# Smaller weight loads and separate tiles for the modulation sums in a hybrid encoder block

## The chip, the cores and the metric

The kernel runs on one core of a Trainium2 chip. The metric is the device time of one execution in microseconds; before the change it is the median of three runs.

## The reference

One encoder layer on 256 tokens of width 2048, in float32:

```python
mod = silu(c) @ ada_w + ada_b                 # c: (1, 2048), ada_w: (2048, 6*2048)
shift_m, scale_m, gate_m, shift_f, scale_f, gate_f = split(mod, 6)
h = rms_norm(x, norm_mix_w) * (1 + scale_m) + shift_m
proj = h @ w_in                               # 18512 columns
# branch A: bidirectional chunkwise mLSTM, 4 heads      -> y_a = (...) @ w_branch_a
# branch B: bidirectional gated delta rule, 16 heads    -> y_b = (...) @ w_branch_b
x = x + gate_m * ((g_a * y_a + g_b * y_b) @ w_out)
hf = rms_norm(x, norm_ffn_w) * (1 + scale_f) + shift_f
gt, up = split(hf @ w_gate_up, 2)             # 2 x 5632 columns
x = x + gate_f * ((silu(gt) * up) @ w_down)
return rms_norm(x, norm_final_w)
```

All weights together are some 450 MB, each read once. `mod` needs the whole of `ada_w`, six parts of 2048 x 2048, which are called here parts 0 to 5.

## The kernel before

**Products.** A float32 product is made of three passes: a weight tile `raw` is split into a rounded high part `wh` (on ScalarE) and the rest `wl` (on VectorE, `wl = raw - wh`), the activations likewise, and TensorE multiplies high with high, high with low and low with high. Two helpers do this. `fjob` takes 16 blocks of 128 x 128 weights as the stationary side and leaves the result with features on partitions (tiles `acc_b` and `acc_a`). `tjob` moves weights of 512 columns past stationary activations; it walks over chunks `u` of 4 x 128 rows in two halves `k0` (0 and 2), each of 12 matmuls. Both read their weights by loads of 1 MB on the SP queue into tiles with the tag `raw`, of which there are three; each such tile gives two halves. `wh` and `wl` have three tiles each, of half the size.

**Modulation sums.** Parts 0 and 1 of `mod` are made in the opening, by two loads `ra` of 1 MB for each of 16 blocks of rows, beside a weight load of 1 MB, `raw0`, which feeds the first 16 products (`first`, line 507). Parts 2 to 5 are made in the background by `ada_part`: a block of 128 x 2048 of the transposed `ada_w` is loaded and VectorE multiplies it with `silu(c)`, broadcast to all partitions (`row_c`), and sums over the row in the same instruction (line 124). Its tile also has the tag `raw`, so these loads and the weight loads share three tiles:

```python
for b in range(KB):
    raw = st.tile([P, D], F32, tag="raw", bufs=3, name=f"ada{part}_{b}")
    nc.sync.dma_start(raw, ada4[part - 2, b])
    V.scalar_tensor_tensor(raw, raw, 1.0, row_c[:, :D], ALU.mult, ALU.mult,
                           accum_out=mod[:, c0 + b : c0 + b + 1])
    yield True
```

**Order.** The Python program lays out the work as generators. `sums(n)` takes n steps of the background list; `pump()` is called by the jobs and calls `sums` every second or fourth time (`every[0]`), or not at all. `fills` holds projection jobs that are put between the short steps of the recurrent branches. The instructions then go through a planner, which may change their order on an engine except where `order(...)` keeps it; on the chip each engine, and the SP queue, runs its own list in order. A tile is given to its next user when the last reader of the user before has ended, so a load waits in the SP queue for the instruction that frees its tile. The stages in order of time (us from the start of the span): opening to about 130; gates; the delta rule's heads with the `b`, `a`, `z`, `v`, `o`, `m` projections as filling, to about 976; the mLSTM heads with the branch projections `yb` and `ya`, to about 1229; the output projection `o` (four groups `g` of 512 columns, with `residual`), to about 1328; the second normalisation, then the FFN: `gt` and `up` to about 1815, `d` to about 2040; the last normalisation.

In the output projection the steps of the background are written out by hand: at half `i` of group `g`, `sums()` is called if `i` is in a given list, and at `g == 3, i == 4` the rest is drained, since the second normalisation needs parts 3 and 4.

Of the kernel before, what the change touches and what calls it, by code (L numbers as in the profile page):

```python
# [15 lines left out]
P = 128  # L16
# [8 lines left out]
KD = 11  # L25
GRP = 4
N0 = 4 + 3 * GRP


PK_ADAB = 0  # L30
# [22 lines left out]
def hybrid_block(ctx: ExitStack, tc: tile.TileContext, xr, nfr, crow, pk_d, cst_d, ada2, ada4, win0, winb, wint, wba, wbb, wo, wgu, wd, out, dbg=None):  # L53
# [31 lines left out]
    def order(ins, yes=True):  # L85

        return tc.keep_in_program_order(ins) if yes else ins
# [6 lines left out]
    pk = cp.tile([P, PK_N], F32, name="pk")  # L94
    cst = cp.tile([P, CS_N], F32, name="cst")
    cp.tile([P, 20], F32, name="edge")
    c1 = st.tile([1, D], F32, tag="raw", bufs=3, name="c1")
    S.dma_start(c1, crow.unsqueeze(0))
    S.dma_start(cst, cst_d)
    S.dma_start(pk, pk_d)  # L100
    ident = cst[:, CS_ID : CS_ID + P]
# [9 lines left out]
    V.memset(row_c[:, D:], 1.0)  # L111
    def c_row(g):
        pc_ = acc_ps.tile([P, 512], F32, tag="acc", name=f"crow{g}")
        order(PE.matmul(pc_, ones[0:1], c1[:, g * 512 : (g + 1) * 512], start=True, stop=True))
        order(S.activation(row_c[:, g * 512 : (g + 1) * 512], pc_, AF.Silu))


    def ada_part(part, row_c):

        c0 = part * KB  # L120
        for b in range(KB):
            raw = st.tile([P, D], F32, tag="raw", bufs=3, name=f"ada{part}_{b}")
            nc.sync.dma_start(raw, ada4[part - 2, b])
            V.scalar_tensor_tensor(raw, raw, 1.0, row_c[:, :D], ALU.mult, ALU.mult, accum_out=mod[:, c0 + b : c0 + b + 1])  # L124
            yield True
        V.tensor_tensor(mod[:, c0 : c0 + KB], mod[:, c0 : c0 + KB], pk[:, PK_ADAB + c0 : PK_ADAB + c0 + KB], ALU.add)
        yield True


# [16 lines left out]
    def fjob(name, src, done):  # L146

        ps = acc_ps.tile([P, 512], F32, tag="acc", name=f"acc_{name}")
        o = ps[:, :T]
        raw = st.tile([P, KB, P], F32, tag="raw", bufs=3, name=f"raw_{name}")  # L150
        nc.sync.dma_start(raw, src)
        for k0 in range(0, KB, 8):
            wh = st.tile([P, 8, P], F32R, tag="wh", bufs=3, name=f"wh_{name}_{k0}")
            wl = st.tile([P, 8, P], F32R, tag="wl", bufs=3, name=f"wl_{name}_{k0}")
            S.activation(wh, raw[:, k0 : k0 + 8], AF.Copy)  # L155
            V.tensor_tensor(wl, raw[:, k0 : k0 + 8], wh.bitcast(F32), ALU.subtract)  # L156
            for k in range(8):
                kk = k0 + k
                PE.matmul(o, wh[:, k], both(hh, kk).rearrange("p a b -> p b a"), start=kk == 0, stop=False)  # L159
                PE.matmul(o, wh[:, k], both(hl, kk).rearrange("p a b -> p b a"), start=False, stop=False)  # L160
                PE.matmul(o, wl[:, k], both(hh, kk).rearrange("p a b -> p b a"), start=False, stop=kk == KB - 1)  # L161
            if k0:
                pump()
                done(o.rearrange("p (b a) -> p a b", a=2))
            yield True

    def tjob(name, chunks, xh, xl, done, early=0, by_token=None, steps=1):
# [1 line left out]

        raws = {}

        def halves(u, k0):
            if u not in raws:
                raws[u] = st.tile([P, 4, 512], F32, tag="raw", bufs=3, name=f"raw_{name}_{u}")
                nc.sync.dma_start(raws[u], chunks[u])
            wh = st.tile([P, 2, 512], F32R, tag="wh", bufs=3, name=f"wh_{name}_{u}_{k0}")
            wl = st.tile([P, 2, 512], F32R, tag="wl", bufs=3, name=f"wl_{name}_{u}_{k0}")
            order(S.activation(wh, raws[u][:, k0 : k0 + 2], AF.Copy), early)  # L180
            order(V.tensor_tensor(wl, raws[u][:, k0 : k0 + 2], wh.bitcast(F32), ALU.subtract), early)  # L181
            return wh, wl

        todo = [(u, k0) for u in range(len(chunks)) for k0 in (0, 2)]
# [9 lines left out]
        for n, (u, k0) in enumerate(todo):  # L194
            wh, wl = made.pop(0) if made else halves(u, k0)
            for k in range(2):
                kk = 4 * u + k0 + k
                for t in range(2):
                    order(PE.matmul(ps[t], tok(xh, kk, t), turns(wh[:, k]), start=kk == 0, stop=False), early and steps > 1)  # L199
                    PE.matmul(ps[t], tok(xl, kk, t), turns(wh[:, k]), start=False, stop=False)  # L200
                    PE.matmul(ps[t], tok(xh, kk, t), turns(wl[:, k]), start=False, stop=kk == last)  # L201
# [236 lines left out]
    with ExitStack() as s0:  # L438
# [54 lines left out]
        for b in range(KB):  # L493
            if b:
                ra, raw = loads(b)
                m2 = scale(b, ra)
            order(V.scalar_tensor_tensor(x[:, b], x[:, b], m2[:, 0:1], rows, ALU.mult, ALU.mult))
            if b:
                shift(ra, m2)
            order(S.activation(x[:, b], x[:, b], AF.Identity, bias=m2[:, 1:2]))  # L500
            two = lambda a: a.rearrange("p (a b) -> p a b", a=2)
            order(S.activation(both(hh, b), two(x[:, b]), AF.Copy))
            for bb in ((b - 1,) if b < KB - 1 else (b - 1, b)):
                if bb >= 0:
                    order(V.tensor_tensor(both(hl, bb), two(x[:, bb]), both(hh, bb).bitcast(F32), ALU.subtract))
            for o in range(N0):
                PE.matmul(  # L507
                    first[o], raw[:, o], x[:, b], start=b == 0 and o % 2 == 0, stop=b == KB - 1 and o % 2 == 1
                )


# [608 lines left out]
    for g in range(4):  # L1120
# [239 lines left out]
```

## Time and profile before

| | us |
|---|---|
| median of 3 runs (2050.05 to 2060.24) | 2050.77 |
| the profiled execution | 2056.24 |
| its span, first to last instruction | 2054.3 |
| mean granted TensorE clock | 0.986 |
| DMA moved, mean over the span | 236 GB/s |

The page gives for each engine the busy time and its share of the span, for stretches the clock that was granted to TensorE, for groups of instructions the mean duration and what ended the idle time before them, and for DMA issues the time from issue to landing. PE is TensorE, PEld its weight loads, DVE VectorE, ACT ScalarE, POOL GpSimd; SPq is the queue from which SP issues loads. "DVE x <- ACT y" means that VectorE's instruction on x waited for ScalarE's on y. L124 is line 124 of the kernel before.

### The profile page before, as it was taken

Reading aid. Unit: us, or ns where it says so; the run is one execution under the profiler, and the core shown is the slowest. Engines: PE = TensorE matmul, PEld = TensorE weight load, DVE = VectorE, ACT = ScalarE, POOL = GpSimd, SP = SyncE. Lnnn points to the kernel's source line nnn. Section 1 sums busy time; section 2 is a strip of 40 time slices with the busy share of each in tenths; the row PEclk is TensorE's granted clock in tenths of the full one; section 3 lists DMA queues with packets and bytes.
Section 4 is the critical chain, followed back from the end, with each engine's and each line's share of the span. In section 5 each row is a group of like instructions: output and inputs, shape, how many; then the busy total and the mean of one; then the engine's idle time right before and its main releaser. Section 6 shows DMA issues by size and latency. Waiting matters only on the chain.

```text
span 2054.3 us, 27035 instructions
## 1 busy us (share of the span) xinstructions
PE 1968.2 (96%) x10374; PEld 1707.0 (83%) x10374; DVE 1394.8 (68%) x2059; ACT 1054.0 (51%) x1584; POOL 106.1 (5%) x205
## 2 busy tenths in 40 slices
PE   8999989999998899999999999889999999999998
PEld 6777779988987898899878787678888888888886
DVE  5787777786888588765667778766656665555554
ACT  3147547856774677466443443364444444444443
POOL 0002210010101010100200000000000000000000
PEclk9999999999999999999999999999999999999999
DMA  9986664566765565666987578756766766555654
GB/s 400 420 321 211 173 216 146 173 190 221 240 224 178 194 207 211 232 247 241 361 295 263 211 264 315 271 184 240 255 243 245 254 238 221 192 204 204 205 203 143
DMA packets 78962, 485.64 MB, mean 236 GB/s; under 512 B 10585, under 2 KB 15969, under 8 KB 24433
## 3 DMA queue, kind: packets, MB, share of 16 engines
q1 hardware_dynamic: 63360, 450.95, 60.9%
q0 software_dynamic: 8160, 17.88, 4.0%
q10 hardware_dynamic: 7314, 15.10, 1.9%
q8 instruction: 81, 1.33, 0.3%
q14 instruction: 47, 0.39, 0.0%
HBM read 467.07 MB, written 16.82 MB: 236 GB/s over the span
## 4 chain that ended last, share of the span: by engine, by line
PE 67%; DVE 13%; DMA 11%; ACT 5%; issue 3%; POOL 1%; ACTq 0%; SPq 0%; DVEq 0%; POOLq 0%
PE acc_up L201 4%; PE acc_up L199 4%; PE acc_up L200 4%; PE acc_d L200 4%; PE acc_d L201 4%; PE acc_d L199 4%; PE acc_gt L200 3%; PE acc_gt L201 3%; PE acc_gt L199 3%; DMA ra<-ada 3%; PE acc_b L161 2%; PE acc_b L159 2%; PE acc_b L160 2%; DMA ada<-ada 2%; PE acc_yb L201 1%
## 5 line engine op out<-in xcount | busy, mean ns | idle before, releaser
L181 DVE TENSOR_TENSOR wl_d<-raw_d,wh_d 128x1024 fp32r<-128x1024 f32 x88 | 107.8, 1225 | 109.1 <-ACT wh_d L180 109.1
L181 DVE TENSOR_TENSOR wl_up<-raw_up,wh_up 128x1024 fp32r<-128x1024 f32 x88 | 107.7, 1225 | 100.4 <-ACT wh_up L180 100.4
L159 PE MATMUL acc_b<-hh,wh_b 128*128 128x256 f32 x576 | 164.1, 285 | 5.8 <-ACT wh_b L155 5.8
L181 DVE TENSOR_TENSOR wl_gt<-raw_gt,wh_gt 128x1024 fp32r<-128x1024 f32 x88 | 107.8, 1225 | 83.2 <-ACT wh_gt L180 83.2
L161 PE MATMUL acc_b<-hh,wl_b 128*128 128x256 f32 x576 | 161.7, 281 | 2.0 <-DVE wl_b L156 2.0
L124 DVE SCALAR_TENSOR_TENSOR ada<-ada,crow 128x2048 f32<-128x2048 f32 x64 | 146.4, 2287 | 25.0 <-DMA ada<-ada 24.8
L160 PE MATMUL acc_b<-hl,wh_b 128*128 128x256 f32 x576 | 160.4, 279 | 0.0
L180 ACT ACTIVATE wh_d<-raw_d 128x1024 fp32r<-128x1024 f32 x88 | 92.9, 1056 | 127.9 <-PE acc_d L200 119.2
L180 ACT ACTIVATE wh_gt<-raw_gt 128x1024 fp32r<-128x1024 f32 x88 | 92.9, 1056 | 118.6 <-PE acc_gt L200 71.0
L180 ACT ACTIVATE wh_up<-raw_up 128x1024 fp32r<-128x1024 f32 x88 | 92.9, 1055 | 108.9 <-PE acc_up L200 78.2
L199 PE MATMUL acc_gt<-wh_gt,hfh 128*128 128x512 f32 x352 | 135.4, 385 | 0.0
L200 PE MATMUL acc_gt<-wh_gt,hfl 128*128 128x512 f32 x352 | 134.7, 383 | 0.1
L201 PE MATMUL acc_gt<-wl_gt,hfh 128*128 128x512 f32 x352 | 133.7, 380 | 0.0
L199 PE MATMUL acc_up<-wh_up,hfh 128*128 128x512 f32 x352 | 133.5, 379 | 0.0
L201 PE MATMUL acc_up<-wl_up,hfh 128*128 128x512 f32 x352 | 133.5, 379 | 0.0
L200 PE MATMUL acc_up<-wh_up,hfl 128*128 128x512 f32 x352 | 133.5, 379 | 0.0
L200 PE MATMUL acc_d<-wh_d,ffl 128*128 128x512 f32 x344 | 131.0, 381 | 0.0
L199 PE MATMUL acc_d<-wh_d,ffh 128*128 128x512 f32 x344 | 131.0, 381 | 0.0
L201 PE MATMUL acc_d<-wl_d,ffh 128*128 128x512 f32 x344 | 130.5, 379 | 0.0
L507 PE MATMUL first<-x,raw 128*128 128x256 f32 x512 | 114.5, 382 | 7.4 <-ACT x L500 6.8
L159 PEld LDWEIGHTS acc_b<-hh,wh_b 128*128 128x128 f32 x576 | 112.5, 195 | 6.4 <-ACT wh_b L155 6.3
L507 PEld LDWEIGHTS first<-x,raw 128*128 128x128 f32 x512 | 96.1, 190 | 25.8 <-ACT x L500 12.4
(369 smaller groups left out, 5275.9 us busy)
## 6 DMA issues: line engine op xcount, KB each, us to landing
ada<-ada SPq DMA_DIRECT2D x64, 1024.0 KB, 5.0
raw_gt<-wgu SPq DMA_DIRECT2D x44, 1024.0 KB, 5.0
raw_up<-wgu SPq DMA_DIRECT2D x44, 1024.0 KB, 4.9
raw_d<-wd SPq DMA_DIRECT2D x44, 1024.0 KB, 4.9
raw_b<-winb SPq DMA_DIRECT2D x36, 1024.0 KB, 5.4
ra<-ada SPq DMA_DIRECT2D x32, 1025.0 KB, 15.7
raw<-win SPq DMA_DIRECT2D x16, 1024.0 KB, 14.5
raw_z<-wint SPq DMA_DIRECT2D x16, 1024.0 KB, 5.8
```

The lines of the kernel that those rows point to most:

```text
L124: V.scalar_tensor_tensor(raw, raw, 1.0, row_c[:, :D], ALU.mult, ALU.mult, accum_out=mod[:, c0 + b : c0 + b + 1])
L159: PE.matmul(o, wh[:, k], both(hh, kk).rearrange("p a b -> p b a"), start=kk == 0, stop=False)
L160: PE.matmul(o, wh[:, k], both(hl, kk).rearrange("p a b -> p b a"), start=False, stop=False)
L161: PE.matmul(o, wl[:, k], both(hh, kk).rearrange("p a b -> p b a"), start=False, stop=kk == KB - 1)
L180: order(S.activation(wh, raws[u][:, k0 : k0 + 2], AF.Copy), early)
L181: order(V.tensor_tensor(wl, raws[u][:, k0 : k0 + 2], wh.bitcast(F32), ALU.subtract), early)
L199: order(PE.matmul(ps[t], tok(xh, kk, t), turns(wh[:, k]), start=kk == 0, stop=False), early and steps > 1)
L200: PE.matmul(ps[t], tok(xl, kk, t), turns(wh[:, k]), start=False, stop=False)
L201: PE.matmul(ps[t], tok(xh, kk, t), turns(wl[:, k]), start=False, stop=kk == last)
L507: PE.matmul(first[o], raw[:, o], x[:, b], start=b == 0 and o % 2 == 0, stop=b == KB - 1 and o % 2 == 1)
```

## The change

Weights come in loads of 512 KB, one for each half, into four tiles `raw` of 512 KB (before, three of 1 MB). The modulation sums are made in halves of 1024 columns into `mh`, whose two columns are added at the end of a part together with the bias. Their tiles have the tag `ada`: two of 512 KB, and six in the pool of the output projection while that runs; the load of step n + 1 stands in the program ahead of the sum of step n. `pump()` is called after each half, so a step is half a sum at twice as many calls. The lists in the output projection go from 3 + 4 + 4 + 3 whole steps to 6 + 8 + 8 + 5 half steps. In the opening, `raw0` comes as two loads, the first into a `raw` tile, the second into a `wl` tile, and the row `c` as two loads. The tiles of these tags take 48 KB per partition before and after, outside the output projection's pool, which grows by 24 KB.

```diff
+NR = 4
+NW = 3
...
-    c1 = st.tile([1, D], F32, tag="raw", bufs=3, name="c1")
-    S.dma_start(c1, crow.unsqueeze(0))
+    c1 = [st.tile([1, D // 2], F32, tag="raw", bufs=NR, name=f"c1_{i}") for i in range(2)]
+    for i in range(2):
+        S.dma_start(c1[i], crow.unsqueeze(0)[:, i * D // 2 : (i + 1) * D // 2])
...
+    ada_in = [st, 2]
     def ada_part(part, row_c):
         c0 = part * KB
-        for b in range(KB):
-            raw = st.tile([P, D], F32, tag="raw", bufs=3, name=f"ada{part}_{b}")
-            nc.sync.dma_start(raw, ada4[part - 2, b])
-            V.scalar_tensor_tensor(raw, raw, 1.0, row_c[:, :D], ALU.mult, ALU.mult, accum_out=mod[:, c0 + b : c0 + b + 1])
+        mh = cp.tile([P, 2, KB], F32, tag="mh", bufs=1, name=f"mh{part}")
+        cols = [slice(i * D // 2, (i + 1) * D // 2) for i in range(2)]
+        def load(b, i):
+            raw = ada_in[0].tile([P, D // 2], F32, tag="ada", bufs=ada_in[1], name=f"ada{part}_{b}_{i}")
+            nc.sync.dma_start(raw, ada4[part - 2, b][:, cols[i]])
+            return raw
+        todo = [(b, i) for b in range(KB) for i in range(2)]
+        raw = load(*todo[0])
+        for n, (b, i) in enumerate(todo):
+            if n + 1 < len(todo):
+                ahead = load(*todo[n + 1])
+            V.scalar_tensor_tensor(raw, raw, 1.0, row_c[:, cols[i]], ALU.mult, ALU.mult, accum_out=mh[:, i, b : b + 1])
+            raw = ahead
             yield True
-        V.tensor_tensor(mod[:, c0 : c0 + KB], mod[:, c0 : c0 + KB], pk[...], ALU.add)
+        V.tensor_tensor(mh[:, 0], mh[:, 0], pk[...], ALU.add)
+        V.tensor_tensor(mod[:, c0 : c0 + KB], mh[:, 0], mh[:, 1], ALU.add)
         yield True
...
     def fjob(name, src, done):
-        raw = st.tile([P, KB, P], F32, tag="raw", bufs=3, name=f"raw_{name}")
-        nc.sync.dma_start(raw, src)
         for k0 in range(0, KB, 8):
+            raw = st.tile([P, 8, P], F32, tag="raw", bufs=NR, name=f"raw_{name}_{k0}")
+            nc.sync.dma_start(raw, src[:, k0 : k0 + 8])
...
+            pump()
             if k0:
-                pump()
                 done(o.rearrange("p (b a) -> p a b", a=2))
...
     def tjob(...):
         def halves(u, k0):
-            if u not in raws:
-                raws[u] = st.tile([P, 4, 512], F32, tag="raw", bufs=3, name=f"raw_{name}_{u}")
-                nc.sync.dma_start(raws[u], chunks[u])
+            raw = st.tile([P, 2, 512], F32, tag="raw", bufs=NR, name=f"raw_{name}_{u}_{k0}")
+            nc.sync.dma_start(raw, chunks[u][:, k0 : k0 + 2])
...
-            if k0:
-                pump()
-                if u == len(chunks) - 1:
-                    done(ps)
+            pump()
+            if k0 and u == len(chunks) - 1:
+                done(ps)
...
         def loads(b):                                      # the opening
-            raw = st.tile([P, N0, P], F32, tag="raw", bufs=3, name=f"raw0_{b}")
+            raw = [
+                st.tile([P, N0 // 2, P], F32, tag=("raw", "wl")[i], bufs=(NR, NW)[i], name=f"raw0_{b}_{i}") for i in range(2)
+            ]
...
-            order(nc.sync.dma_start(raw, win0[b]))
+            for i in range(2):
+                order(nc.sync.dma_start(raw[i], win0[b][:, i * N0 // 2 : (i + 1) * N0 // 2]))
...
     wp = pool(sw, "wp")                                    # the output projection
+    ada_in[:] = [wp, 6]
...
-            if i in ((4, 6, 7), (1, 2, 4, 6), (1, 2, 4, 6), (1, 2, 4))[g]:
+            if i in ((2, 3, 4, 5, 6, 7), range(8), range(8), range(5))[g]:
                 sums()
...
     background.append(ada_part(5, row_c))
+    ada_in[:] = [st, 2]
     sw.close()
```

More of the change, by code (lines that the diff above doesn't have):

```diff
@@ L167, in tjob @@
     def tjob(name, chunks, xh, xl, done, early=0, by_token=None, steps=1):
-        raws = {}
         def halves(u, k0):
-            if u not in raws:
-                raws[u] = st.tile([P, 4, 512], F32, tag="raw", bufs=3, name=f"raw_{name}_{u}")
[L177 to L181, printed above, removed]
+            raw = st.tile([P, 2, 512], F32, tag="raw", bufs=NR, name=f"raw_{name}_{u}_{k0}")
+            nc.sync.dma_start(raw, chunks[u][:, k0 : k0 + 2])
+            wh = st.tile([P, 2, 512], F32R, tag="wh", bufs=NW, name=f"wh_{name}_{u}_{k0}")
+            wl = st.tile([P, 2, 512], F32R, tag="wl", bufs=NW, name=f"wl_{name}_{u}_{k0}")
+            order(S.activation(wh, raw, AF.Copy), early)
+            order(V.tensor_tensor(wl, raw, wh.bitcast(F32), ALU.subtract), early)
             return wh, wl
@@ L507, in hybrid_block @@
                 PE.matmul(
-                    first[o], raw[:, o], x[:, b], start=b == 0 and o % 2 == 0, stop=b == KB - 1 and o % 2 == 1
+                    first[o], raw[o // (N0 // 2)][:, o % (N0 // 2)], x[:, b], start=b == 0 and o % 2 == 0, stop=b == KB - 1 and o % 2 == 1
                 )
```

12 lines of the change are left out of this document (6 added, 6 removed).

## Prediction

> **What bounds the kernel now.** I read the page first (shares, clock, queues), then the table by stage, then in the stages where TensorE is not full the waits of TensorE and of the SP queue, and last the chain at those places.
>
> ```profile
> span 2054.3 us, 27035 instructions
> PE 1968.2 (96%) x10374; PEld 1707.0 (83%) x10374; DVE 1394.8 (68%) x2059; ACT 1054.0 (51%) x1584; POOL 106.1 (5%) x205
> ```
>
> The span is 2054.3 us, and TensorE is busy for 96% of it; its busy time counts the ends of overlapping matmuls, so a waiting TensorE shows in the stages. By stage (the columns are the stretch, its length, the busy time of PE, PEld, DVE, ACT, POOL, the granted clock, the DMA share and GB/s):
>
> ```profile
> 20.00:125.00 105.00, 99.97 (x449) 83.98 (x448) 74.94 (x84) 12.94 (x28) 0.00 (x0) 1.00 1.01 420
> 714.40:721.20 6.80, 6.23 (x27) 5.93 (x28) 5.17 (x7) 3.00 (x5) 0.00 (x0) 0.50 0.51 178
> 1083.00:1086.40 3.40, 2.84 (x11) 2.31 (x12) 2.65 (x8) 1.35 (x3) 0.00 (x0) 0.51 0.79 265
> 1304.90:1311.70 6.80, 6.12 (x14) 4.88 (x15) 5.77 (x6) 2.60 (x5) 0.00 (x0) 0.50 0.77 284
> 1232.00:1312.00 80.00, 71.41 (x297) 56.69 (x296) 64.53 (x71) 30.47 (x41) 0.00 (x0) 0.96 0.86 320
> 1386.00:2040.00 654.00, 654.00 (x3056) 568.37 (x3055) 373.10 (x355) 289.17 (x306) 0.00 (x0) 1.00 0.63 220
> ```
>
> Three kinds of stage are to be seen. The opening (20 to 125) moves 420 GB/s with the DMA engines full: it is bound by bytes, which the change leaves as they are. From 1386 to 2040, the FFN, TensorE is never idle and has its full clock: 654 us in which no better load can gain anything. In between lie the stages where TensorE waits now and then, and where its clock falls to a half for 3.4 or 6.8 us right after such a wait. Only there can the change gain. Who holds it up:
>
> ```profile
> PE acc_o L199 <- ACT wh_o L180: 4.0, 5, 1.9
> PE acc_o L201 <- DVE wl_o L181: 3.9, 3, 2.3
> SPq L123 <- DVE wl_o L181: 38.5, 12, 5.1
> SPq L177 <- DVE ada L124: 33.7, 12, 7.0
> ```
>
> These are the waits from 1229 to 1312, the output projection (total us, times, longest): TensorE waits 7.9 us for split weights, and the SP queue issues each weight load only when a modulation sum has given its slot back, and each modulation load only when a weight split has. The two kinds of load pass the same three tiles of 1 MB to each other. The chain shows one turn of it:
>
> ```profile
> 1282.62 6.41 DMA raw_o<-wo
> 1289.14 1.06 ACT wh_o L180
> 1291.37 1.23 DVE wl_o L181
> 1292.62 6.97 DMA ada<-ada
> 1299.68 2.30 DVE ada L124 x2
> 1306.80 0.43 PE acc_o L199
> 1311.90 0.22 PE acc_o L199
> ```
>
> A weight load of 6.41 us, then a modulation load of 6.97 us that VectorE, which runs in order, stands waiting for with the next weight split queued behind it; TensorE then restarts at one matmul in 0.43 us, twice the 0.22 it has at 1311.90.
>
> **The change, part by part.**
>
> *Own tiles for the modulation.* Weights no longer wait for sums nor sums for weights, and each sum's data is asked for a step before it is used. The output projection loses at most its two waits, 4.0 + 3.9 = 7.9 us, and half of the 6.80 us at clock 0.50, 3.4 us: 11.3 us. What is late next is VectorE: it is busy 64.5 of the 80 us from 1232 to 1312, and 80 - 11.3 = 68.7 leaves it little room. I take 8 us, because three things run close to full there at once. Thirteen full sums lie in this stage:
>
> ```profile
> 1229.00:1340.00 111.00, 29.86 (x26) 0.95 0.78 288
> L124 DVE SCALAR_TENSOR_TENSOR ada<-ada,crow x64: 2266/2286/2294, 494.4 to 1694.8; 128x2048 f32<-128x2048 f32 x64
> L124 DVE DVE_READ_ACCUMULATOR ada<-ada,crow x64: 80/83/91, 496.6 to 1697.0; 128x1 f32 x64
> ```
>
> The first row counts VectorE's instructions on the modulation tile alone: 26, two for each sum. The new schedule asks for 6 + 8 + 8 + 5 = 27 half steps there where 13 sums and an addition (14 steps) stood, so nothing is left over for the drain at the end. With one half sum for each half chunk, a g of the loop moves 8 x 1.05 MB in 8 x 12 matmuls x 0.22 us = 21 us, 400 GB/s, against the 420 that the opening reaches: the six tiles that fill ahead are what makes that bearable.
>
> *616 to 820.* TensorE's waits there, the chain, and the clock after the first stall:
>
> ```profile
> PE acc_b L159 <- ACT wh_b L155: 5.8, 3, 2.8
> PE acc_b L161 <- DVE wl_b L156: 1.8, 3, 0.8
> 683.49 2.30 DVE ada L124 x2
> 685.81 5.32 DMA raw_b<-winb
> 708.48 2.21 DVE ada L124 x2
> 700.80:704.20 3.40, 3.40 (x18) 3.40 (x18) 0.82 (x2) 3.25 (x8) 0.00 (x0) 0.50 0.48 166
> ```
>
> The first stall is the slot: load raw_b leaves at 685.81, the moment the sum ends. Its price is half of the first row, 2.9 us, and half of 3.40 at clock 0.50, 1.7. The second, at 708, is not: there a sum of 2.21 us only stands on VectorE ahead of the convolution; cut in two it holds 1.1 us less. Together 2.9 + 1.7 + 1.1 = 5.7 us, out of at most 5.8 + 1.8 + 5.1 = 12.7 (both stretches at half clock). I take 5.7.
>
> *1030 to 1229.* Here one sum stalls TensorE by itself:
>
> ```profile
> 1073.41 7.30 DMA ada<-ada
> 1080.81 2.30 DVE ada L124 x2
> PE pxa L976 <- DVE hal L981: 2.6, 1, 2.6
> ```
>
> VectorE waits for a load issued at 1073.41, and the head's output behind it waits with it. Asked for a step ahead, the load has landed: 2.6 us, and half of the 3.40 at clock 0.51, 1.7: 4.3 us.
>
> The skill speaks to the clock: the Trainium skill, "TensorE: Matmul & The Clock Gate", Part 1, says that the clock halves after a full idle window of about 3.4 us. The trace here halves it right after waits whose longest is 2.3 us (wl_o), 2.8 us (wh_b) and 2.6 us (hal). By that rule alone the clock's 3.4 + 1.7 + 1.7 us would not hang on these waits, and the gain below would be up to 6.8 us smaller; I follow the trace.
>
> *Halves instead of wholes on VectorE.* No row has the half sum. A split of half the size lies near:
>
> ```profile
> L181 DVE TENSOR_TENSOR wl_o<-raw_o,wh_o x30: 1215/1222/1226, 1224.0 to 1319.3; 128x1024 fp32r<-128x1024 f32 x30
> ```
>
> Two at 1222 are 2444 against 2286: 0.16 us more a sum, with a second accumulator read 0.24, over 64 sums 15 us of VectorE at most, and below zero nothing is to be had. On the path lies only what falls where VectorE is last: the 8 sums of 616 to 820 and the 13 of the output projection, 21 x 0.24 = 5 us at most. Consecutive instructions overlap at their ends, and I take 1 us. The three extra additions on 16 columns are nothing beside that.
>
> *Half loads.* A load of 512 KB exists, a smaller one too; ahead of them what SP needs for one issue (ns):
>
> ```profile
> L123 SPq DMA_DIRECT2D ada<-ada x64: 327/328/328, 487.3 to 1689.7; - x64
> DMA to landing us min/median/max: 4.2/5.3/5.7
> DMA to landing us min/median/max: 2.1/2.4/2.7
> DMA to landing us min/median/max: 4.7/4.9/6.5
> q1 hardware_dynamic: 63360, 450.95, 60.9%
> q10 hardware_dynamic: 7314, 15.10, 1.9%
> ```
>
> The landings are in this order those of gta (512 KB), outT (256 KB), raw_up (1 MB). A straight line from 2.1 to 4.7 gives 3.0 us for 512 KB; gta has 4.2. So a half lands after 3.0 to 4.2 us, two in turn cost 1.2 to 3.7 us more than one whole of 4.7. None of it is on the path while the tiles run ahead. Four tiles are four halves, 4 x 12 x 0.22 = 10.5 us of TensorE; of these the split takes 1.06 + 1.23 and the landing up to 4.2, which leaves 4 us. Before, three wholes held up to six halves, but a sum took one of them away. So in the FFN I cost it at nothing: the cover is these 4 us. In the opening the bytes are the bound, so a slower rate is paid in full. The ends of that price are 0 (the ACT queue, with 15.10 MB in 7314 packets, so 2 KB each, moved them in 1.9% of the span, 387 GB/s; the SP queue, 450.95 MB in 60.9%, 360 GB/s) and 16 x 1.24 = 20 us (each of the 16 extra loads pays its fixed part in turn). The 420 GB/s of the opening speak for the low end, since loads of 4.7 us one after another would reach 223. I take 1 us. SP has room: an issue takes 0.33 us, and in the FFN one weight load is issued for each half chunk, 12 x 0.22 = 2.6 us of matmuls.
>
> *No cost, one answer.* The second half of the opening's weights sits in the three wl tiles until its matmuls end; the first job's third split needs the last of them, and gets it when the opening's matmuls end, which VectorE's next work awaits anyway. The row of c in two loads puts one more issue (0.33 us) ahead of the constants, in an opening that the bytes bound. Six tiles of 4 KB in the projection's own pool displace finished tiles only.
>
> **The sum.** -8 - 5.7 - 4.3 + 1 + 1 = -16 us. The profiled execution took 2056.24 us with its span of 2054.3; that would become 2040. It stood 5.5 us above the median of the runs, 2050.77, so the forecast for the median is 2035 us.
>
> **The rivals.**
>
> *VectorE is late next (2047 us).* The loads come in time, but in the projection VectorE's 64.5 us plus 13 x 0.24 = 3 become the bound with the residuals between, and in 616 to 820 the stalls turn out to be VectorE's order. Then only the 4.3 us of 1030 to 1229 remain. For it: the second stall at 708, and 81% of VectorE in the projection. Against it: the SP rows, where 33.7 us of waiting end with a sum. 2050.8 - 4 = 2047.
>
> *SP blocks itself (2065 us, the other side).* SP issues in order. With two rings a modulation load that waits for its tile can hold back weight loads whose tile is free; with one ring the two could not disagree. Modulation loads do wait long:
>
> ```profile
> SPq L123 <- DVE wl_b L156: 23.3, 4, 10.0
> ```
>
> From 4 us on, the room that four halves leave, such a wait reaches TensorE: one of 10.0 costs 6. Four such in 616 to 820 are 24 us; with the gain of 5.7 gone and the others kept, -10 + 24 = +14 gives 2065. Against it: a tile is asked for only after VectorE's last sum but one, and VectorE runs sums and splits in the order in which they were planned.
>
> *Each half load pays its fixed part (2062 us).* If the 1.24 us of a second load is paid in turn wherever DMA is the bound, the opening grows by 20 instead of 1 and the projection, which needs 400 GB/s, keeps its waits: -16 + 19 + 8 = +11. The row of 420 GB/s in the opening speaks against it: there three loads lie over each other. The Trainium skill, "DMA: Bandwidth & Descriptors", Rules for kernel authors, asks for at least 1 MiB in a load for the best bandwidth, and its formula of 2.0 us plus bytes over 436 GB/s gives, as an estimate, 4.4 us for 1 MB and 3.2 for 512 KB, so 2.0 us more for two halves; by it the opening would grow by 32 us. The trace agrees with the fixed part for a single load and not for overlapped ones.
>
> *The change doesn't do what it says (2051 us).* If loads leave no earlier than now, because weights were asked for as soon as possible all along, nothing moves.
>
> **How the numbers follow.** My forecast, the slots as the limit, gets 0.64, with its own range of 2018 to 2041: at one end 11.3 + 12.7 + 4.3 = 28 us with no cost, and one more stall like that of 1030 to 1229 in a stage that I have not costed; at the other 10 us, where VectorE gives back a third. VectorE late next gets 0.18, no effect 0.03, SP blocking itself 0.10, the fixed part 0.05. A measurement tells some 0.5% from no change here, 10 us: below 2040.5 is faster, above 2061 slower. The forecast's range lies nearly all in faster, with 0.01 beyond it and 0.03 of the VectorE case added: 0.66. The two middle cases make 0.20, the two others 0.14. The range takes in the first two cases and no effect and leaves out most of the last two: 2015 to 2058.
>
> **What would show it.** Right: no SP wait that names a sum ahead of a weight load; TensorE's waits for wh_o and wl_o below 3 us, and no stretch at half clock at the end of the projection; the pxa wait gone; the half sum at about 1.2 us; the opening still at about 420 GB/s; the FFN unchanged at full clock. Wrong: an opening longer by over 5 us (the fixed part), SP waits on modulation tiles of over 4 us followed by waits for raw weights (SP blocks itself), or VectorE without gaps in the projection (late next).

## Result: 2.6% slower, and the profile after

The changed kernel took 2108.22 us, the median of 4 runs (2103.10 to 2111.43), beside 2051.57 us for the kernel before on the same chip: a ratio of 1.026, 95% interval 1.0235 to 1.0281. The profiled execution took 2103.10 us. The forecast of 2035 us and its range were wrong, and on the wrong side.

From the page of the changed kernel, the span, the row of busy times, the sums' group (its last column is VectorE's idle time just before them) and the lines of two loads (KB each, median us from issue to landing); then, from the view of one source line, where in the span the sums lie (first and last start ahead of the semicolon):

```profile
span 2101.1 us, 27968 instructions
PE 1981.3 (94%) x10374; PEld 1720.9 (82%) x10374; DVE 1395.6 (66%) x2191; ACT 1057.0 (50%) x1585; POOL 106.2 (5%) x205
L139 DVE SCALAR_TENSOR_TENSOR ada<-ada,crow 128x1024 f32<-128x1024 f32 x128 | 155.9, 1220 | 67.2 <-DMA ada<-ada 66.8
ada<-ada SPq DMA_DIRECT2D x128, 512.0 KB, 6.0
raw_up<-wgu SPq DMA_DIRECT2D x88, 512.0 KB, 4.4
```
```profile
L139 DVE SCALAR_TENSOR_TENSOR ada<-ada,crow x128: 1194/1221/1229, 139.7 to 1455.5; 128x1024 f32<-128x1024 f32 x128
```

Two things stand out. VectorE waits 66.8 us for the sums' loads; in the kernel before it was 24.8 us, in 18 places (total, times, longest):

```profile
DVE ada L124 <- DMA ada<-ada: 24.8, 18, 2.7
```

And the first sum starts at 139.7 us, where before it started at 494.4. The code says nothing of the kind: the background list still begins to be taken where it did. The planner, which may move every instruction that is not kept in its order, has taken sums and loads forward to the end of the opening. It could, because their tiles are now their own: in the kernel before each sum's tile stood in line between two weight tiles of the same ring, so a sum could not go far from its place.

The table by stage, of VectorE's work on the sums alone (length, busy time and count, the granted clock, DMA share, GB/s), first of the kernel before, then of the changed one:

```profile
138.00:420.00 282.00, 0.00 (x0) 0.98 0.59 185
420.00:820.00 400.00, 36.70 (x32) 0.98 0.63 210
```
```profile
138.00:360.00 222.00, 44.17 (x72) 0.93 0.80 261
138.00:420.00 282.00, 57.52 (x94) 0.94 0.78 252
138.00:616.00 478.00, 88.11 (x144) 0.94 0.76 244
616.00:820.00 204.00, 0.00 (x0) 0.98 0.61 176
1256.00:1340.00 84.00, 30.64 (x50) 0.98 0.89 336
1340.00:1386.00 46.00, 15.98 (x26) 0.81 0.80 259
```

Two instructions belong to each half sum. The 72 half sums that the code has between 494 us and the output projection (parts 2 and 3 and the first quarter of part 4) stand at 138 to 616 us. The projection keeps its 25, whose tiles come from the projection's own pool. Part 5 begins in the second normalisation (around 1340 to 1386, clock 0.81), where the code has none of it, and ends at 1457 us.

What it cost can be read from when TensorE starts its last (or first) matmul on a tile (us; "held" is the experiment below that keeps the sums in place):

| | before | changed | held |
|---|---|---|---|
| opening's products, last | 138 | 139 | 139 |
| first `p` of the delta rule's heads | 312 | 359 | 309 |
| `acc_b`, last | 804 | 838 | 781 |
| `acc_ya`, last | 1225 | 1256 | 1202 |
| `acc_o`, last | 1328 | 1353 | 1299 |
| `acc_up`, first | 1365 | 1402 | 1336 |
| `acc_up`, last | 1811 | 1858 | 1782 |
| `acc_d`, last | 2044 | 2091 | 2015 |

47 us are lost before the first head, 16 come back up to 1256, where sums are missing now, 6 more in the output projection, then 12 are lost in the normalisation and 10 in gate and up. The stage of the first loss, all engines, first before, then changed, and after that, of the changed kernel, the wait of VectorE from 130 to 420:

```profile
138.00:360.00 222.00, 207.03 (x1093) 177.09 (x1092) 168.45 (x339) 141.31 (x237) 32.91 (x61) 0.97 0.60 189
138.00:313.00 175.00, 161.07 (x709) 132.71 (x708) 134.79 (x276) 103.66 (x160) 29.87 (x55) 0.96 0.63 197
```
```profile
138.00:360.00 222.00, 189.07 (x882) 157.16 (x880) 185.56 (x367) 119.55 (x180) 30.05 (x55) 0.93 0.80 261
```
```profile
DVE ada L139 <- DMA ada<-ada: 23.0, 18, 3.3
```

Before, VectorE is busy 134.8 us until the heads start at 312, out of 175 us. In the changed kernel it is busy 185.6 of the 222 us to 360, 44.2 of them with sums, and stands waiting for their loads for up to 23 more: 209 us of 222. So VectorE is what has the least room here. The chain of waits in that stage of the changed kernel (start, us, what) shows how it goes:

```profile
277.31 6.59 DMA ada<-ada
283.93 0.07 DVE ada L139
...
285.08 0.08 DVE ada L139
285.16 0.27 DVE utmp L647
285.43 1.13 DVE wl_mb L195
286.56 0.29 DVE uu L653
286.85 0.07 SPq L191
286.92 0.05 issue
286.97 8.24 DMA ada<-ada
```

A sum's load of 6.59 us, the sum, one step of the head's inverse (`utmp`, `uu`), one split, and the next load of 8.24 us. The inverse is a chain of small steps on which the first head waits, and here it moves on by a few of them for each load. The sum's load leaves the SP queue right behind a weight load (`SPq L191`), which had waited for its own tile. The output projection of the changed kernel, by contrast, all engines:

```profile
1259.00:1339.00 80.00, 72.82 (x323) 60.88 (x321) 68.91 (x107) 34.42 (x45) 0.00 (x0) 0.98 0.90 342
```

TensorE is busy 72.82 of 80 us and does 323 matmuls there, where before it was 71.41 us and 297: what I had expected of this stage is there, and is buried under the rest.

### The profile page after: what moved, and what is told of

Read it like the earlier page. It is cut to its first block, busy times and chain, and to the rows that moved or that the text cites. A ratio compares the mean times of both kernels' runs of the same rounds, so it can differ in the third digit from the quotient of the medians.

```text
span 2101.1 us, 27968 instructions
## 1 busy us (share of the span) xinstructions
PE 1981.3 (94%) x10374; PEld 1720.9 (82%) x10374; DVE 1395.6 (66%) x2191; ACT 1057.0 (50%) x1585; POOL 106.2 (5%) x205
## 4 chain that ended last, share of the span: by engine, by line
PE 63%; DMA 20%; DVE 10%; issue 3%; ACT 3%; POOL 1%; SPq 0%; DVEq 0%; ACTq 0%; POOLq 0%
DMA ada<-ada 7%; DMA ra<-ada 6%; PE acc_d L215 4%; PE acc_d L214 4%; PE acc_d L213 4%; PE acc_up L215 3%; PE acc_up L213 3%; PE acc_up L214 3%; PE acc_gt L213 3%; PE acc_gt L214 3%; PE acc_gt L215 3%; PE acc_b L176 2%; PE acc_b L178 2%; PE acc_b L177 2%; PE acc_o L215 2%
## 5 line engine op out<-in xcount | busy, mean ns | idle before, releaser
L139 DVE SCALAR_TENSOR_TENSOR ada<-ada,crow 128x1024 f32<-128x1024 f32 x128 | 155.9, 1220 | 67.2 <-DMA ada<-ada 66.8
L195 DVE TENSOR_TENSOR wl_d<-raw_d,wh_d 128x1024 fp32r<-128x1024 f32 x88 | 107.8, 1225 | 109.1 <-ACT wh_d L194 109.1
L195 DVE TENSOR_TENSOR wl_up<-raw_up,wh_up 128x1024 fp32r<-128x1024 f32 x88 | 107.5, 1225 | 105.5 <-ACT wh_up L194 105.5
L195 DVE TENSOR_TENSOR wl_gt<-raw_gt,wh_gt 128x1024 fp32r<-128x1024 f32 x88 | 107.6, 1225 | 86.3 <-ACT wh_gt L194 86.3
L178 PEld LDWEIGHTS acc_b<-hh,wl_b 128*128 128x128 f32 x576 | 112.6, 195 | 2.9 <-DVE wl_b L173 2.6
```

The costliest lines, as they stand in the source:

```text
L139: V.scalar_tensor_tensor(raw, raw, 1.0, row_c[:, cols[i]], ALU.mult, ALU.mult, accum_out=mh[:, i, b : b + 1])
L195: order(V.tensor_tensor(wl, raw, wh.bitcast(F32), ALU.subtract), early)
```

## The experiments

Line numbers are those of the changed kernel unless said otherwise. "Held" means that `order(...)` stands around an instruction, which keeps it behind the one ahead of it in the program.

### The sums held to their place

```diff
-            V.scalar_tensor_tensor(raw, raw, 1.0, row_c[:, cols[i]], ...
+            order(V.scalar_tensor_tensor(raw, raw, 1.0, row_c[:, cols[i]], ...
```

> The changed kernel with one edit: each modulation sum on VectorE is held behind the VectorE instruction that stands before it in the program, so the planner cannot move it forward; tiles, loads and halves stay. In the changed kernel the first sum runs at about 142 us instead of 494, ahead of work that VectorE is late with. Theory A (the sums were moved ahead, and VectorE does them and waits for their loads where it sets the pace): about 2035 us, the blind forecast, between 2020 and 2050, and VectorE waits for modulation loads under 15 us instead of 66.8. Theory B (two rings in the in-order SP queue block each other): the rings are still there, so 2090 or more. Theory C (loads of 512 KB are dearer): they are still there, so 2090 or more.

Measured: 2030.97 us (2027.00 to 2032.48), against 2055.34 us before on that chip: 0.9889, interval 0.9868 to 0.991. One call changes 2.6% slower into 1.1% faster. Theory A holds; B and C, which needed 2090 us or more, fall. Of the held kernel: where the sums lie; the wait for their loads, and the waits in the projection (1206 to 1301) and of the head that stalled on `hal`; and the FFN:

```profile
L139 DVE SCALAR_TENSOR_TENSOR ada<-ada,crow x128: 1184/1218/1226, 494.2 to 1671.0; 128x1024 f32<-128x1024 f32 x128
```
```profile
DVE ada L139 <- DMA ada<-ada: 2.5, 1, 2.5
PE acc_o L215 <- DVE wl_o L195: 6.4, 3, 3.4
PE pxa L992 <- DVE hs L985: 0.2, 1, 0.2
```
```profile
1357.00:2011.00 654.00, 654.00 (x3056) 568.78 (x3055) 375.80 (x386) 289.21 (x306) 0.00 (x0) 1.00 0.70 221
```

The sums start at 494.2 again, VectorE waits for one load in 128, the stall of 2.6 us on `hal` is gone (what `pxa` still waits, 0.2 us, is for `hs`), and the FFN takes the same 654 us without a gap. From 138 us to the first head at 309, VectorE does nearly the work of the kernel before, without a sum:

```profile
138.00:309.00 171.00, 157.00 (x708) 129.22 (x707) 134.63 (x277) 104.26 (x161) 29.93 (x55) 0.99 0.68 203
```

The held kernel also answers the rival of the prediction in which SP blocks itself. The SP queue's waits with a sum's load for one of the sums' tiles, first in the changed kernel, then in the held one:

```profile
SPq L131 <- DVE ada L139: 80.0, 46, 4.2
SPq L131 <- DVE ada L139: 97.9, 96, 4.5
```

They are longer in total in the kernel that is 77 us faster, so they are not what the changed kernel lost its time by.

### Which part's move costs what

```diff
-            order(V.scalar_tensor_tensor(raw, raw, ...))
+            order(V.scalar_tensor_tensor(raw, raw, ...), part < 5)
```

> The changed kernel with the sums of parts 2, 3 and 4 held in place and those of part 5 left free. It splits the loss. By theory A part 5 moves from the FFN into the second normalisation, where the changed kernel's lead over the kernel before grows by 13 us (31 to 47 us between the end of the branch projections and the end of the FFN): some 15 to 22 us more than the run with all sums held, so about 2055. By B and C, near 2100.

Measured: 2053.90 us, a single run. With part 5 alone free, 23 us are lost against the held kernel, and from there to the changed kernel, where parts 2 to 4 are free too, another 54 (2108.22 - 2053.90). The 23 us are close to what theory A expected. The loss of part 5 lies where the table has it: the first `acc_up` starts at 1352 here, 16 us after the held kernel's, and the last at 1809, 27 after.

### One ring for weights and sums, sums free

```diff
-NR = 4
+NR = 6
-            raw = ada_in[0].tile([P, D // 2], F32, tag="ada", bufs=ada_in[1], ...)
+            raw = st.tile([P, D // 2], F32, tag="raw", bufs=NR, ...)
```

> The changed kernel without tiles of their own for the sums: weights in halves and sums in halves share one ring of six tiles of 512 KB (24 KB per partition as before), also in the output projection; nothing is held by hand. The ring gives its tiles in program order, so the sums stay near their places. Theory A: 2040 to 2060, close to the kernel before. Theory B: also near 2050, since there is one ring. Theory C (512 KB loads): 2090 or more. Together with the first run it separates B from A.

Measured: 2125.07 us (2123.84 to 2127.34), 1.0346 (1.0327 to 1.0365): slower than the changed kernel itself. So a shared ring, by itself, was no cure, and theories A and B fell. The time is in the range of theory C, but the first experiment, with the same loads, rules C out. VectorE's wait for the sums' loads, and SP's weight loads behind sums:

```profile
DVE ada L139 <- DMA ada<-ada: 203.8, 89, 7.2
SPq L191 <- DVE ada L139: 189.4, 61, 8.2
```

The ring does stop the long move: no sum stands before 420 us. But VectorE waits 203.8 us. In VectorE's order a half sum now stands 1 to 28 weight splits ahead of where the held kernel has it, 6 in the mean (number 1 behind 106 splits instead of 110, number 17 behind 136 instead of 164). In the changed kernel the 72 ahead of the projection stand 104 to 218 splits ahead.

### The same ring, sums held

The edit is that ring, with the `order(...)` of the first experiment.

> The kernel with one shared ring of six 512 KB tiles (no own tiles for the sums, which took 2125 us), with each half sum now held to its place in VectorE's program. Theory 'order': what made the shared ring slow is where the planner put the sums between the splits (VectorE waited 203.8 us in 89 places for their loads); held, the ring costs little: 2030 to 2055 us, and VectorE's waits for those loads fall below 30 us. Theory 'ring': weights and sums pass the same tiles to each other (the SP queue waited 189 us in 61 places with a weight load for a sum's tile), whatever the order: it stays at 2090 to 2130 us, and that SP row stays above 120 us.

Measured: 2041.48 us (2039.00 to 2043.53, 10 runs), 0.9937 (0.9919 to 0.9955). The theory of the order holds: in the same tiles, holding the sums is worth 2125 - 2041 = 84 us. VectorE's waits for the sums' loads are too small to show, and the row of SP that the other theory kept above 120 us reads:

```profile
SPq L191 <- DVE ada L139: 65.5, 64, 4.9
```

### The kernel before, with its sums held

```diff
-            V.scalar_tensor_tensor(raw, raw, 1.0, row_c[:, :D], ...
+            order(V.scalar_tensor_tensor(raw, raw, 1.0, row_c[:, :D], ...
```

> The kernel before with nothing changed but that each whole sum is held to its place in VectorE's program. It is the control of the holding itself. Theory 'own tiles' (the gain of the held change, 24 us, comes from separate tiles and halves): the shared ring already held the sums in their place, so this is within 8 us of the kernel before, 2047 to 2063 us. Theory 'holding' (holding sums is what gains, and the tiles nothing): 2025 to 2040 us.

Measured: 2044.27 us (2039.64 to 2049.22, 10 runs), 0.995 (0.993 to 0.9971). It lies between the two theories: even in the kernel before, the planner had moved sums by up to 3 weight splits ahead of the held order, and holding them gains 10 us. VectorE's wait for their loads falls from 24.8 us to this (line numbers of the kernel before):

```profile
DVE ada L124 <- DMA ada<-ada: 4.4, 7, 0.9
```

### Whole loads, one own tile for the sums

The kernel before with three tiles divided, two for the weights and one for the sums, free and then held:

```diff
-            raw = st.tile([P, D], F32, tag="raw", bufs=3, name=f"ada{part}_{b}")
+            raw = st.tile([P, D], F32, tag="ada", bufs=1, name=f"ada{part}_{b}")
...
-        raw = st.tile([P, KB, P], F32, tag="raw", bufs=3, name=f"raw_{name}")
+        raw = st.tile([P, KB, P], F32, tag="raw", bufs=2, name=f"raw_{name}")
```

> The kernel before with one edit: the sums, whole and in 1 MB loads, get one tile of their own, and the weights keep two tiles of 1 MB (same memory). Theory A: the sums are no longer tied to the weights' ring and move ahead here too, first sum near 140 us instead of 494, and the time rises by 30 us or more, to 2080 or above. Theory C: no load got smaller, so near 2051, at most some us more for the shorter weight ring.

> Whole 1 MB loads: one own tile for the sums, two for the weights, as in the run of 2189 us, now with each sum held to its place. Theory 'the planner moves sums with tiles of their own': most of the 135 us go, 2050 to 2085 us, the rest being the weights' two tiles. Rival, the two weight tiles are the cause: it stays above 2130 us.

Measured, one run each: 2188.89 us free and 2148.07 us held. Free, the sums move here too, with whole loads (46 instructions on their tile from 138 to 420 us, none before). Holding them gives back 41 us, not the 105 or more that I expected, and the rival's bound of 2130 us is met: most of the loss stays with the sums in place, and fits the weights' two tiles of 1 MB. What waits in the held one:

```profile
PE acc_b L159 <- ACT wh_b L155: 21.9, 15, 2.4
PE acc_z L199 <- ACT wh_z L180: 18.9, 10, 4.1
```

With two wholes the next load leaves only when both halves of a tile are split. With four halves for the weights and two for the sums, the same bytes, the held kernel takes 2036 us (two own tiles throughout, below). So it is with halves that tiles can be taken from the weights; that run also asks for each sum's load a step ahead, which is not separated from the halves here.

### Early sums with short loads

```diff
-            raw = ada_in[0].tile([P, D // 2], F32, tag="ada", ...)
-            nc.sync.dma_start(raw, ada4[part - 2, b][:, cols[i]])
+            raw = ada_in[0].tile([P, D // 16], F32, tag="ada", ...)
+            nc.sync.dma_start(raw, ada4[part - 2, b][:, i * D // 2 : i * D // 2 + D // 16])
...
+            dump = st.tile([P, D // 2], F32, tag="dump", bufs=1, ...)
+            V.scalar_tensor_tensor(dump.rearrange(...), raw.unsqueeze(1).to_broadcast([P, 8, D // 16]), ...)
```

> The changed kernel with sums free to move, but each half sum loads only 64 KB (128 columns, read eight times over by the same VectorE instruction of 1024 columns); so the work on VectorE and its early place stay, and only the loads are short; the sums' values are not those of the reference. Theory 'the price of the early place is VectorE standing in line for loads' (66.8 us in 43 places in the changed kernel): those waits fall below 15 us and the time to 2035 to 2060 us. Rival 'the price is VectorE's extra work in stages that are short of it': the time stays at 2085 to 2110 us. DMA has 58.7 MB less to move, which may take some us off the output projection in both cases.

Measured: 2083.15 us, a single run; in neither theory's range, and just below the rival's. The wait halves, it doesn't go (the group on the page, and of the short loads the time to landing):

```profile
L140 DVE SCALAR_TENSOR_TENSOR dump<-ada,crow 128x1024 f32<-128x1024 f32 x128 | 155.7, 1217 | 33.1 <-DMA ada<-ada 32.6
```
```profile
DMA to landing us min/median/max: 1.8/3.2/9.6
```

34 us less of waiting came with 25 us less of time. The first head starts at 360 us as in the changed kernel: in that stage the planner put even more sums, 57.45 us from 138 to 360 instead of 44.17, so more work stands there instead. Both theories seem to hold in part: an early sum costs its own time where VectorE is what the next stage waits for, and the wait for its load besides. How much of each is not separated, since the order changed as well.

### Loads held, sums free

```diff
-            nc.sync.dma_start(raw, ada4[part - 2, b][:, cols[i]])
+            order(nc.sync.dma_start(raw, ada4[part - 2, b][:, cols[i]]))
```

> The changed kernel with own tiles, in which the load of each half sum is held to its place in the SP queue's program and the sum itself is free. In the planned VectorE order a sum then stands one to eleven weight splits ahead of where the held kernel has it (sum 64 behind 302 splits there, behind 300 here; sum 32 behind 164 and 164+11), as in the shared ring that took 2125 us. Theory 'far moves cost, near ones don't, because the weights have tiles of their own': VectorE waits under 60 us for these loads and the time is 2030 to 2055 us. Rival 'each sum that stands ahead of its data stops VectorE, whichever tiles it uses': VectorE waits over 120 us for them and the time is 2080 to 2125 us.

Measured: 2132.59 us (2132.30 to 2137.92), 1.0383 (1.0349 to 1.0416). The rival won, with a time even above its range: a short move (1 to 26 splits, 4 in the mean) costs more than the long one. VectorE waits 162.8 us in 74 places. One of them in the FFN, on VectorE (start, us, what, idle time before it), the load on the SP queue, and the wait of TensorE from 1560 to 1590:

```profile
1573.53 1.23 DVE L139 SCALAR_TENSOR_TENSOR ada<-ada,crow 128x1024 f32<-128x1024 f32 x1 [4.63 <-DMA ada<-ada]
1574.68 0.08 DVE L139 DVE_READ_ACCUMULATOR ada<-ada,crow 128x1 f32 x1
1574.68 1.28 DVE L1227 TENSOR_TENSOR sg<-sg,acc_up 128x512 f32<-128x512 f32 x2
```
```profile
1565.24 0.43 SPq L131 DMA_DIRECT2D ada<-ada  x1
```
```profile
PE pxf L1233 <- DVE sg L1227: 4.8, 1, 4.8
```

The load leaves at 1565.24, as late as the code has it; the sum stands in line for it and ends its wait at 1573.53; the product `sg` that TensorE's `pxf` needs stands behind the sum; TensorE waits 4.8 us. Gate and up of the FFN, which had no gap before, lose 49 us; VectorE waits 70.6 us there for sums' loads, and TensorE's `pxf` 33.7 us for `sg`. First before (1365 to 1811), then here:

```profile
1365.00:1811.00 446.00, 446.00 (x2098) 388.21 (x2097) 264.16 (x242) 199.16 (x210) 0.00 (x0) 1.00 0.66 236
```
```profile
1398.00:1893.00 495.00, 460.05 (x2099) 398.54 (x2098) 266.93 (x275) 199.92 (x210) 0.00 (x0) 0.97 0.67 213
```

### Two own tiles throughout

```diff
-    ada_in[:] = [wp, 6]
```

> The held kernel (2031 us) without the change of the sums' tiles from two to six in the output projection. Theory 'the six tiles that fill ahead make the projection's rate bearable': the projection loses the 6 us that it gained, 2034 to 2042 us, and VectorE waits over 3 us for sums' loads there. Rival 'the separation is what counts, two tiles do': 2027 to 2034 us.

Measured: 2035.56 us (2035.03 to 2042.07), 0.9918 (0.9888 to 0.9948). VectorE's wait for sums' loads in the projection becomes 10.5 us in 11 places, against 2.5 in one place. That is as the theory of the six tiles has it, and in the two traces the projection takes 101 us instead of 97; but the intervals of the two ratios overlap, so the 4.6 us between the medians are likely and not shown.

### Twice the sums' work, in place

```diff
             order(V.scalar_tensor_tensor(raw, raw, ...))
+            order(V.scalar_tensor_tensor(raw, raw, ...))
```

> The held kernel (2031 us) with every half sum's VectorE instruction issued twice in place, so 128 x 1.22 = 156 us more work on VectorE, at the same places and with the same loads; the sums' values are not those of the reference. Theory 'it is the place and the waiting, not the work': VectorE is busy some 69% of the span and takes it up for a good part, 2035 to 2065 us. Rival 'VectorE's work is what bounds wherever a sum stands': each us is paid, over 2100 us. The moved sums of the changed kernel put 44 us of this work ahead of 360 us and paid about 47 us there, so a cost under 0.3 us for each us of work speaks for the place.

Measured: 2069.35 us, a single run: 38 us for 156 us of work, 0.25 us for each. Between the two traces it is 42 us: 24 up to the last `acc_ya` (1226 against 1202), 18 in the output projection (1341 against 1299 at the last `acc_o`), where VectorE has the least room. TensorE's wait for the weight splits there, from 1220 to 1345 (6.4 us in the held kernel):

```profile
PE acc_o L216 <- DVE wl_o L196: 17.4, 9, 5.3
```

So more work in the sums' own places costs about a quarter of its time. In the changed kernel 44 us of early sums, with the waits that they brought, cost 47.

### The splits held too

```diff
-            V.tensor_tensor(wl, raw, wh.bitcast(F32), ALU.subtract)
+            order(V.tensor_tensor(wl, raw, wh.bitcast(F32), ALU.subtract))
...
-            order(V.tensor_tensor(wl, raw, wh.bitcast(F32), ALU.subtract), early)
+            order(V.tensor_tensor(wl, raw, wh.bitcast(F32), ALU.subtract))
```

> The held kernel (2031 us) with the weight splits on VectorE held to their place as well. Theory 'the planner moves only the sums to where their data is late': splits gain nothing by it, 2028 to 2045 us. Rival 'splits stand ahead of their data too': 2005 to 2025 us. Third, the splits need the planner's freedom to run ahead beside the head's chains of small instructions: over 2050 us.

Measured: 2278.85 us (2274.28 to 2282.43), 1.1103 (1.1067 to 1.114). The third way, by far. VectorE now waits for TensorE and ScalarE in the heads' and the FFN's chains, with splits standing behind:

```profile
DVE cv L309 <- ACT cv L307: 61.1, 29, 3.8
DVE r L760 <- PE pb L759: 48.2, 15, 6.3
DVE sg L1227 <- PE acc_up L215: 46.1, 11, 5.0
```

The planner's freedom is worth much for the splits and costs much for the sums.

## Why the prediction was wrong, and what of it was right

**The step that failed** is "each sum's data is asked for a step before it is used", on which the gains of the own tiles rest, together with the places at which these gains and VectorE's halves were costed ("the 8 sums of 616 to 820"). Both took the order of the code for the order on the chip, as the sentence against the rival "SP blocks itself" shows: "VectorE runs sums and splits in the order in which they were planned". The planner, however, plans anew, and what had tied a sum to its place was the ring that the change took away. In the changed kernel no sum lies in 616 to 820, the first starts at 139.7 us instead of 494.4, and VectorE waits 66.8 us for the sums' data instead of 24.8. The count for the projection did come out: 27 half steps were asked for, and 25 half sums lie there. No term of the sum looked for a move, and no rival did: the cost ahead of 360 us (47 us), in the normalisation (12) and in gate and up (10) lies in stages that I had not costed, or costed at nothing.

**What held it in place before, and what does now.** Shown: with own tiles the sums start at 139.7 us, with the shared ring or the hold after 420; holding them takes the changed kernel from 2108 to 2031 us. Holding the loads alone stops the long move as well (first sum at 488.7 us, with own tiles). Shown too: it is not the far move as such. Loads in place and sums a few splits ahead cost 2133 us, more than the far move's 2108. Each sum that stands ahead of its data stops VectorE, and all that is behind it.

**The terms, against the held kernel.** It is the change as I had costed it, and took 24.4 us off the kernel before where I had -16. That its 2031 us lie near my 2035 is partly luck: some 10 us come from the hold, which no term had. The stages below are of one trace each, and one kernel's executions differ by several us.
- Output projection, -8: from the last `acc_ya` to the last `acc_o` 103 us became 97. The size was nearly right, the signs half: SP has no row left in which a weight load waits for a sum's tile, but TensorE's waits for `wl_o` are 6.4 us where I asked for under 3. VectorE is late next, as its rival said, without taking the gain away. I had also misread what the clock follows. The wait of 2.3 us on `wl_o`, which I put right ahead of the stretch at half clock, had ended at 1279.30, and the stretch began at 1304.90, behind waits of 1.85 and 1.16 us. The held kernel has such a stretch too, of 3.4 us instead of 6.8, behind a wait of 2.59 us that ended at 1236.14:

```profile
1236.60:1240.00 3.40, 3.40 (x10) 2.68 (x9) 3.40 (x6) 0.05 (x1) 0.00 (x0) 0.51 0.86 254
```

- 616 to 820, -5.7: from the first `p` to the last `acc_b` 492 us became 473. Holding alone, in the kernel before, gives 9 us of it (483). The shared ring of halves, held, comes to 474, so the rest goes with the halves and needs no own tiles, to which I had put most of it.
- The stall on `hal`, -4.3: 2.6 us of waiting are gone, as forecast. They are gone in the changed kernel and in the held shared ring too, and down to 1.6 us in the kernel before with its sums held; so this is not the own tiles' doing alone.
- Halves on VectorE, +1: the half sum takes 1.218 us, 2 x 1.218 + 2 x 0.083 = 2.60 against 2.286 + 0.083 = 2.37, 0.23 a sum, against 0.24 forecast. What it costs has no run of its own; at the 0.25 us for each us of work that the run with twice the work shows, 64 x 0.23 = 15 us would cost some 4 us, an estimate, more than my 1.
- Half loads in the FFN, at nothing: right, TensorE waits nowhere in the held kernel's FFN. The time to landing was off, though: the straight line rested on `outT`, which is a store and no load, and halves of the weights landed after 4.4 us in the changed kernel and 4.6 in the held one (`raw_up`, where 1 MB took 4.9), above my 3.0 to 4.2.
- Opening, +1: 138 became 139, at 417 GB/s in the changed kernel (row below). The Trainium skill, "DMA: Bandwidth & Descriptors", Rules for kernel authors, asks for loads of 1 MiB and more; by its formula (Anatomy of one DMA, fitted there to loads issued by GpSimd, while these are SP's) the opening would have grown by an estimated 32 us. The measured 1 us, with a third of the opening's bytes in halves, decides against paying a fixed part for each of several loads under way at once. For a single load such a part is there: half the bytes landed only 0.3 to 0.5 us sooner in the FFN.

```profile
20.00:125.00 105.00, 100.24 (x447) 84.39 (x445) 75.48 (x84) 12.63 (x28) 0.00 (x0) 0.99 1.02 417
```

**The gain, taken apart.** All with sums held: three shared wholes 2044.27, six shared halves 2041.48, four and two own halves 2035.56, with six in the projection 2030.97. The ends differ clearly; each step between is near what the intervals can tell. Of the 24 us, 10 are what the hold gives in the kernel before, which is no part of the change. In the output projection the traces give 104, 105, 101 and 97 us in this order, so there, and only there, the own tiles seem to pay.

**Open.** Why the planner puts a sum ahead of its load can't be seen in a trace; its own idea of how long a load takes was not tried. How much of the changed kernel's loss is waiting and how much the sums' own time is not separated either: the run with short loads changed the order as well.

## What to carry to other kernels

A ring of tiles that two streams share is also an order between them. Whoever divides it must ask what else keeps that order, and read in the new trace first where each stream's first and last instruction lie. Background work on an engine that runs in order belongs behind work whose data is there: hold it to a place, and leave free what fills gaps, as the splits here. And a gain that a changed kernel doesn't show may still be in it: the held version, 2030.97 us, beats both kernels.

## What the runs showed of the hardware

A small load isn't a quick one in every case: the 64 KB loads landed after 1.8 us at best, 3.2 us in the median and 9.6 us at worst, in the queue that also carried the 512 KB weight loads. So cutting a load to an eighth took away only half of VectorE's waiting (66.8 to 32.6 us). The Trainium skill, "DMA: Bandwidth & Descriptors", Queues, rings and completion order, says that descriptors are consumed in ring order on each DMA engine. The 9.6 us would fit a load that stands behind others; no run here shows what it stood behind.
